# Seven products for eight in the second feed-forward, and two new prices in the planner of a two-layer transformer block

## The chip, the cores and the metric

The kernel runs on one core of a Trainium2 chip. The core has a matrix engine (TensorE, PE in the profile; its weight loads are listed apart as PEld), VectorE (DVE), ScalarE (ACT), GpSimd (POOL) and SyncE (SP), which here issues all transfers. The metric is the device time of one execution in microseconds. Of the kernel before there are three runs: 1750.07, 1753.08 and 1755.17 us, median 1753.08.

## The reference

Two layers work on 512 latent tokens (`x`) and, in the first layer only up to its end, 256 context tokens (`ctx`), with 1024 channels; everything is float32. The mixer has three groups of heads. What matters here is the feed-forward and that layer 1 does it for the latent tokens alone:

```python
def swiglu(h, w1, w3, w2):
    return (jax.nn.silu(h @ w1) * (h @ w3)) @ w2       # 1024 -> 2816 -> 1024

for layer in range(2):
    last = layer == 1
    ...
    x = x + mx[2] * (ox @ w_out[layer])
    x = x + mx[5] * swiglu(modulate(rmsnorm(x, g_ffn[layer]), mx[3], mx[4]), w_ff1[layer], w_ff3[layer], w_ff2[layer])
    if not last:
        ctx = ctx + ...                                # the same for the context tokens
return rmsnorm(x, g_final)
```

## The kernel before

**Products.** A float32 product is made as three fp32r matmuls: each operand is split into a rounded part `hi` and a rest `lo` (a cast on ACT or DVE, then a subtraction on DVE), and hi·hi, hi·lo and lo·hi are added up in PSUM. `split_w` does that for weights. In attention the probabilities are transposed by TensorE (128 rows and columns) and multiplied with the values in plain float32 with 64 output rows, two heads side by side (`pv_pair`, and the same in `attn_c`); such a group is followed by work of 128 output rows again.

**Feed-forward** (from `ncol` to the end of the layer's loop in `dit_block`). The 2816 hidden channels are 22 steps (`FT`) of 128. A step loads and splits the columns of w1 and w3 (`ff_weights`), makes two up projections (`ff_up`, 24 matmuls of 512 columns each in layer 1, where the 512 tokens are the moving side), gates them (`silu` on ACT, product on DVE), and splits the gated tile (`ff_gate`). The down projection of the step before lies between (`ff_w2`, `ff_down`): for each of the four tiles of 128 tokens six matmuls of 512 columns, whose two PSUM tiles DVE adds into the sums `ys`. The last `FF_TAIL` = 3 steps have no down projection in the loop; behind it the sums are gated and added to the residual `xf` (`dve_pool`: VectorE or GpSimd), the w2 rows of those three steps are multiplied by the gate in layer 1 and split, and their down projections end the layer tile by tile. In layer 1 the final norm and the store follow each tile.

**The planner** (class `Plan`). The program records its operations in an order written out by hand, with alternatives of engine where it says so (`act_dve`, `dve_pool`). `schedule` then simulates the five engines with the durations of `price` and takes again and again the operation that can start first; among those of one engine the one earliest in program order, less a `boost` for attention scores and softmax. Several matmuls recorded in `together` are one operation. A transfer may go `lead` operations ahead (`LEAD`), and tiles come from pools with a fixed count (`SLOTS`: 41 tiles of 4 KB in `u`; in PSUM two of two banks, four of one). The order that comes out is the order of each engine's instructions, and all are issued in one line (347), so rows are told apart by tile names: `wh`, `wl` are split weights, `sg` the gated tile, `gh`, `gl` its parts, `y` the sums, `S` and `T` PSUM tiles, `pt` transposed probabilities.

Of the kernel before, what the change touches and what calls it, by code (L numbers as in the profile page):

```python
# [28 lines left out]

ORDER = ["dddd P0 P1 ddddB P2 BABeeeeABAeeeeBABABABeeeeeeeeeCAAAACCCCCC",  # L30
         "P1 P0 B P2 ABBBCAACAABCCCAAB"]
FF_TAIL = 3
FF_ADA = "dddd"
QK_AHEAD = 238
ADA_AHEAD = 300
# [5 lines left out]
COLS = {("a", "q"): (0, 384), ("a", "k"): (384, 128),  # L41
        ("b", "q0"): (640, 128), ("b", "q1"): (768, 128), ("b", "k"): (896, 256),
        ("c", "q"): (1408, 384), ("c", "k"): (1792, 128)}
SA = 0.125
SB = 32.0 ** -0.5
SLOTS = {"u": 41, "pt": 4, "s": 7, "y": 24, "rb": 2, "S": 2, "T": 4, "ropeG": 1}
# [1 line left out]

class _Op:
    __slots__ = ("pos", "alts", "deps", "tiles", "dma", "gate", "tag", "boost",  # L50
                 "users", "left", "banks", "ready", "end", "eng", "calls", "at", "cost", "name")


class _Queue:
# [12 lines left out]
class Plan:  # L67
# [100 lines left out]
    def add(self, alts):  # L168
        op = _Op()
        op.pos, op.tag = len(self.ops), self.label  # L170
        if alts[0][1] is None:
            calls = [o for _, _, o in alts]
            op.alts = [(calls[0][0], sum(self.price(*o) for o in calls), calls)]
        else:
            calls = [alts[0][1]]
            op.alts = [(e, self.price(*c), [c]) for e, c, _ in alts]
        op.dma = calls[0][1] == "dma_start"
        op.gate = op.pos - self.lead if op.dma else 0
        op.boost = 0
        deps, tiles, banks = set(), set(), set()  # L180
        for eng, _, args, kw in calls:
            writes = [args[0]] + ([kw["accum_out"]] if "accum_out" in kw else [])
            reads = [a for a in list(args[1:]) + [v for k, v in kw.items() if k != "accum_out"] if self.is_ap(a)]
            if eng == "pe" and self.label.startswith("att") and self.tile_tag.get(args[0].tensor.name) == "S":
                op.boost = QK_AHEAD
            if not op.dma and self.label in ("ada0", "normA0"):
                op.boost = ADA_AHEAD
            if eng != "pe" and self.label.startswith("att") and any(self.tile_tag.get(a.tensor.name) == "S" for a in reads):
                op.boost = SM_AHEAD
            todo = []  # L190
            if eng == "pe" and kw.get("start", True):

                ws, _ = self.acc.setdefault(args[0].tensor.name, ([], []))
                m = sum(self.banks(args[0]))
                deps.update(o for o, mm in ws if mm & m and o < op.pos and self.ops[o].alts[0][0] == "pe")
            for aps, wr in ((reads, False), (writes, True)):
                for ap in aps:
                    name = ap.tensor.name
                    if name in self.given:
                        continue  # L200
                    m = self.region(ap)
                    if ap.space == PSUM:
                        banks.update((name, b) for b in self.banks(ap))
                    ws, rs = self.acc.setdefault(name, ([], []))
                    deps.update(o for o, mm in ws if mm & m)
                    if wr:
                        deps.update(o for o, mm in rs if mm & m)
                    todo.append((name, m, wr))
            for name, m, wr in todo:
                ws, rs = self.acc[name]  # L210
                if wr:
                    ws[:] = [(o, mm) for o, mm in ws if mm & ~m] + [(op.pos, m)]
                    rs[:] = [(o, mm) for o, mm in rs if mm & ~m]
                else:
                    rs.append((op.pos, m))
                if name in self.tile_tag:
                    tiles.add(name)
        deps.discard(op.pos)
        op.deps, op.tiles, op.banks = deps, tiles, banks
        for t in tiles:  # L220
            self.first.setdefault(t, op.pos)
            self.last[t] = op.pos
        self.ops.append(op)

    def schedule(self):
# [17 lines left out]
        free_at = dict.fromkeys(self.real, 0.0)  # L243
        cand = {e: [] for e in self.real}
        dma_free, now, frontier = 0.0, 0.0, 0
        done, order = [False] * n, []

        bank_end = {}
# [12 lines left out]
        while len(order) < n:  # L261
            best = None
            for e in sorted(free_at, key=free_at.get):
# [51 lines left out]
            if op.dma:  # L315
                free_at[e] = now + 0.5
                dma_free = max(now + 1.4, dma_free) + c
                op.end = dma_free + self.AFTER[e]
            else:
                free_at[e] = now + c  # L320
                op.end = now + c + self.AFTER[e]
            for b in op.banks:
                bank_end.setdefault(b, {})[e] = op.end
            order.append(op)
# [26 lines left out]
def dit_block(  # L351
# [293 lines left out]
    for l in range(2):  # L645
# [646 lines left out]
        def halves(ap):  # L1292
            return [ap[:, 512 * hf:512 * hf + 512] for hf in range(2)]

        ys, gs, ada = {}, [], ada_later()
        for ft in range(FT):
            plan.label = f"ffn{l}"
            plan.lead = LEAD["else"] if ft == 0 else LEAD["ff"]
            ws = ff_weights(ft)
            down = 0 < ft <= FT - FF_TAIL  # L1300
            w2 = ff_w2(ft - 1) if down else None
            for ch in FF_ADA if l == 0 and 1 < ft < FT - FF_TAIL else "":
# [9 lines left out]
            for a in range(2):  # L1312
# [3 lines left out]
                for part in range(1 if last else 2):  # L1316
                    if ft:
                        ff_up(ws[a], s, part)
                    if down:
                        k = 2 * a + part  # L1320
                        for r, i in qtiles[2 * a:2 * a + 2] if last else qtiles[FF_CUT[k]:FF_CUT[k + 1]]:
                            if ft == 1:
                                ys[r, i] = U([1024], name="y")
                            for p, yv in zip(ff_down(gs, [w2], r, i), halves(ys[r, i])):
                                if ft == 1:
                                    act_dve.copy(yv, p)
                                else:
                                    dve.tensor_tensor(yv, p, yv, ALU.add)
                if a == 0:
# [10 lines left out]
        w2s = [ff_w2(ft, gated) for ft in range(FT - FF_TAIL, FT)]  # L1340
        for r, i in qtiles:
            xt = xt0[r, i] = U([1024], name="xf")
            sp.dma_start(xt, xscr[NX * r + i])
            for xv, yv, gate in zip(halves(xt), halves(ys[r, i]), gates[r]):
# [95 lines left out]
```

## Time and profile before

| | |
|---|---|
| runs of the kernel before | 1750.07, 1753.08, 1755.17 us |
| the profiled execution: time / span of its instructions | 1754.11 / 1752.3 us |
| PE busy | 1697.7 us, 97% of the span |
| DVE / ACT / POOL busy | 69% / 35% / 12% |
| mean granted TensorE clock | 0.994 of full speed |

The span of instructions is 1.8 us shorter than the execution. Busy time counts from an instruction's start to its modelled end; instructions of one engine overlap a little, so their pace is read from one start to the next. The layers follow one another: layer 0's attention and projections up to about 470 us, its feed-forward to about 1060, layer 1's attention to about 1345, its feed-forward to the end.

### The profile page before, as it was taken

The page shows a single profiled execution, that of the slowest core. Times are in us where ns is not written, and L with a number is a line of the kernel's source. Part 1 is how long each engine was busy: PE and PEld are TensorE (multiplying, and loading weights), DVE is VectorE, ACT ScalarE, POOL GpSimd, SP SyncE. Part 2 cuts the span into 40 slices and gives each one's busy share as a digit, 9 for nine tenths or more (in the row PEclk, how much of TensorE's full clock was granted, in tenths as well). Part 3 has the DMA queues.
Part 4 walks back from the last instruction along what each step waited for, and adds up shares of the span by engine and source line. Part 5 has one row for each costly group of instructions (what it writes and reads, how often), then busy time and mean ns, then how long its engine had stood idle before and what let it go on. Part 6 is the DMA issues. An engine that isn't in the chain of part 4 may idle for free.

```text
span 1752.3 us, 24291 instructions
## 1 busy us (share of the span) xinstructions
PE 1697.7 (97%) x9426; PEld 1361.3 (78%) x9426; DVE 1208.2 (69%) x1950; ACT 615.2 (35%) x1280; POOL 218.1 (12%) x251
## 2 busy tenths in 40 slices
PE   6999898998999999999999999999999999999998
PEld 3787666676898888888888878877777888888886
DVE  3775878675567887576655765778876666676676
ACT  2523867663342122111101133157674411111111
POOL 0252200011000000000000521542001000000022
PEclk9999999999999999999999999999999999999999
DMA  9502220306363544254232342012005632332341
GB/s 314 188 27 84 67 85 20 96 11 171 96 200 101 169 159 148 93 191 136 69 108 89 105 145 72 13 31 68 1 1 157 180 109 75 106 109 81 112 144 48
DMA packets 153278, 182.96 MB, mean 104 GB/s; under 512 B 9316, under 2 KB 121396, under 8 KB 153164
## 3 DMA queue, kind: packets, MB, share of 16 engines
q1 hardware_dynamic: 153164, 181.42, 33.5%
q8 instruction: 74, 1.21, 0.3%
q14 instruction: 40, 0.33, 0.1%
HBM read 163.00 MB, written 9.47 MB: 98 GB/s over the span
## 4 chain that ended last, share of the span: by engine, by line
PE 86%; DVE 7%; issue 2%; POOL 2%; ACT 2%; DMA 2%; SPq 0%; DVEq 0%; POOLq 0%; ACTq 0%
DMA ws__1259<-in_w_out_dram 1%; PE S__1380 L347 0%; PE S__1379 L347 0%; PE S__1756 L347 0%; PE S__1561 L347 0%; PE S__1628 L347 0%; PE S__1881 L347 0%; PE S__1691 L347 0%; PE S__1823 L347 0%; PE S__1495 L347 0%; PE S__1995 L347 0%; PE S__1393 L347 0%; PE S__1967 L347 0%; PE S__1861 L347 0%; PE S__1853 L347 0%
## 5 line engine op out<-in xcount | busy, mean ns | idle before, releaser
L347 POOL TENSOR_TENSOR y__1397<-y__1397,gate__1998 128x512 f32<-128x512 f32 x1 | 1.3, 1297 | 481.0 <-DVE y__1397 L347 481.0
L347 POOL TENSOR_TENSOR ws__3491<-ws__3491,gate__3490 128x512 f32<-128x512 f32 x1 | 1.3, 1284 | 284.8 <-DMA ws__3491<-in_w_ff_dram 284.8
L347 DVE TENSOR_REDUCE t__2138<-sq__2137 128x6 f32<-128x384 f32 x1 | 0.6, 553 | 19.5 <-ACT sq__2137 L347 19.5
L347 ACT ACT_TABLE_LOAD x6 | 7.7, 1283 | 2.6 <-PE S__3040 L347 1.9
L347 ACT ACTIVATE sg__1860<-S__1853 128x768 f32<-128x768 f32 x1 | 0.8, 812 | 21.2 <-PE S__1853 L347 21.2
L347 ACT ACTIVATE sg__1914<-S__1907 128x768 f32<-128x768 f32 x1 | 0.8, 812 | 21.2 <-PE S__1907 L347 21.2
L347 ACT ACTIVATE sg__1940<-S__1933 128x768 f32<-128x768 f32 x1 | 0.8, 812 | 21.2 <-PE S__1933 L347 21.2
L347 ACT ACTIVATE sg__1966<-S__1959 128x768 f32<-128x768 f32 x1 | 0.8, 812 | 21.2 <-PE S__1959 L347 21.2
L347 DVE TENSOR_TENSOR sg__1994<-sg__1994,S__1995 128x768 f32<-128x768 f32 x1 | 1.0, 955 | 10.3 <-PE S__1995 L347 10.3
L347 ACT ACTIVATE sg__1793<-S__1786 128x768 f32<-128x768 f32 x1 | 0.8, 812 | 17.3 <-PE S__1786 L347 17.3
L347 ACT ACTIVATE sg__1665<-S__1658 128x768 f32<-128x768 f32 x1 | 0.8, 812 | 16.6 <-PE S__1658 L347 16.6
L347 PE MATMUL T__115<-wa__116,cstat 128*32 128x128 f32 x8 | 0.7, 418 | 5.7 <-DMA wa__116<-in_w_ada_dram 5.7
L347 ACT ACTIVATE xn__2033<-xf__2011 128x1024 f32<-128x1024 f32 x1 | 1.1, 1066 | 14.2 <-DVE xf__2011 L347 14.2
L347 POOL TENSOR_TENSOR ropeG<-ropeA,gqk 128x64 f32<-128x64 f32 (+1 forms) x12 | 6.0, 531 | 0.1
L347 ACT ACTIVATE sg__3107<-S__3102 128x512 f32<-128x512 f32 x1 | 0.6, 598 | 14.8 <-PE S__3102 L347 14.8
L347 ACT ACTIVATE sg__3459<-S__3454 128x512 f32<-128x512 f32 x1 | 0.6, 599 | 13.9 <-PE S__3454 L347 13.9
L347 ACT ACTIVATE sg__3173<-S__3168 128x512 f32<-128x512 f32 x1 | 0.6, 598 | 13.8 <-PE S__3168 L347 13.8
L347 ACT ACTIVATE sg__3195<-S__3190 128x512 f32<-128x512 f32 x1 | 0.6, 598 | 13.8 <-PE S__3190 L347 13.8
L347 ACT ACTIVATE sg__3217<-S__3212 128x512 f32<-128x512 f32 x1 | 0.6, 598 | 13.8 <-PE S__3212 L347 13.8
L347 ACT ACTIVATE sg__3239<-S__3234 128x512 f32<-128x512 f32 x1 | 0.6, 598 | 13.8 <-PE S__3234 L347 13.8
L347 ACT ACTIVATE sg__3261<-S__3256 128x512 f32<-128x512 f32 x1 | 0.6, 598 | 13.8 <-PE S__3256 L347 13.8
L347 ACT ACTIVATE sg__3283<-S__3278 128x512 f32<-128x512 f32 x1 | 0.6, 598 | 13.8 <-PE S__3278 L347 13.8
(14035 smaller groups left out, 6711.6 us busy)
## 6 DMA issues: line engine op xcount, KB each, us to landing
x__83<-in_x_dram SPq DMA_DIRECT2D x1, 512.0 KB
x__84<-in_x_dram SPq DMA_DIRECT2D x1, 512.0 KB
x__131<-in_x_dram SPq DMA_DIRECT2D x1, 512.0 KB, 5.9
x__136<-in_x_dram SPq DMA_DIRECT2D x1, 512.0 KB, 6.5
x__198<-in_ctx_dram SPq DMA_DIRECT2D x1, 512.0 KB
x__203<-in_ctx_dram SPq DMA_DIRECT2D x1, 512.0 KB
ws__241<-in_w_in_dram SPq DMA_DIRECT2D x1, 512.0 KB
ws__244<-in_w_in_dram SPq DMA_DIRECT2D x1, 512.0 KB
```

The costliest lines, as they stand in the source:

```text
L347: getattr(self.real[op.eng], method)(*args, **kw)
```

## The change

1. **Down projection of layer 1** (`WINO`). Two steps (256 hidden channels) are taken together. The 512 tokens, the 256 channels and the 1024 outputs are each cut in two, and the product of the 2 x 2 blocks is made by seven block products of sums and differences of blocks (Winograd's form of Strassen's method) in place of eight. Each block product is again three fp32r matmuls for each of two tiles of 128 tokens. The seven products are added up over nine pairs of steps in seven tiles (`wino_y`), and `wino_sum` makes the four blocks of the result from them once. `FF_TAIL` becomes 4 in layer 1, so that 18 steps are taken in pairs.
2. **Planner.** fp32r matmuls are priced (n + 32)/2400 us. `shares_port` names the operations that the planner takes to hold one SBUF port in common (all of GpSimd's; VectorE's with two SBUF inputs, and scalar operations and copies from SBUF to SBUF); the planner lets only one of them run at a time. In attention, a TensorE operation whose count of output rows differs from that of the one before starts 0.095 us later, and operations up to 30 positions behind it may go first.
3. **End of both feed-forwards.** Gating the sums and adding them to the residual is VectorE's alone.

```diff
-FF_TAIL = 3
+FF_TAIL = (3, 4)
+WINO = (1,)
+SWITCH = 0.095
+MODE_AHEAD = 30
...
-                return n / 2400 + 0.003 if n >= 256 else 0.213
+                return (n + 32) / 2400 if n >= 256 else 0.213
...
+    def shares_port(self, eng, method, args, kw):
+        if eng == "pool":
+            return method != "dma_start"
+        if eng != "dve" or method == "memset":
+            return False
+        ins = [a for a in args[1:] if self.is_ap(a) and a.space != PSUM and int(np.prod(a.shape[1:])) > 1]
+        if method.startswith("tensor_scalar") or method == "tensor_copy":
+            return bool(ins) and args[0].space != PSUM
+        return len(ins) > 1
...
+                    if e == "pe" and soon is not None and item[0] > soon[1][0] + MODE_AHEAD and soon[0] <= t0 + SWITCH + 1e-9:
+                        break
...
+                    if e == "pe" and op.mode != mode and op.tag.startswith("att"):
+                        at += SWITCH
+                    if op.port[e]:
+                        at = max(at, port)
...
+        def wino_down(Ge, Go, ft, first):
+            n = ncol // 2
+            nt = n // 128
...
+            def product(form, A, B):
+                (ah, al), (bh, bl) = A, B
+                for t in range(nt):
+                    c = slice(128 * t, 128 * t + 128)
+                    p = PT()
+                    with plan.together():
+                        for k, (a, b) in enumerate(((ah, bh), (ah, bl), (al, bh))):
+                            pe.matmul(p, lhsT=a[:, c], rhs=b, start=(k == 0), stop=(k == 2))
+                    if first:
...
+                        act_dve.copy(wino_y[form, t], p)
+                    else:
+                        dve.tensor_tensor(wino_y[form, t], p, wino_y[form, t], ALU.add)
...
+            sa = split_s(a11, [n])
+            sb = split_s(b11, [512])
+            product(1, sa, sb)
+            yield
+            dve.tensor_tensor(S[:, 0], a21, a22, ALU.add)
+            sub(dve, T[:, 0], b12, b11)
+            sub(dve, S[:, 1], S[:, 0], a11)
+            sub(dve, T[:, 1], b22, T[:, 0])
+            s12, t12 = split_s(S, [2, n]), split_s(T, [2, 512])
+            sub(dve, S3[:, 0], a11, a21)
+            sub(dve, T3[:, 0], b22, b12)
+            sub(dve, S3[:, 1], a12, S[:, 1])
+            sub(dve, T3[:, 1], T[:, 1], b21)
+            product(5, pair(s12, 0), pair(t12, 0))
...
+            product(6, pair(s12, 1), pair(t12, 1))
...
+            s34, t34 = split_s(S3, [2, n]), split_s(T3, [2, 512])
+            product(7, pair(s34, 0), pair(t34, 0))
...
+            so2 = split_s(wo2, [1024])
...
+            product(3, pair(s34, 1), pair(so2, 1))
...
+            sgo = split_s(Go[:, 0:2 * n], [2 * n])
...
+            product(4, pair(sgo, 1), pair(t34, 1))
...
+            product(2, pair(sgo, 0), pair(so2, 0))
...
+        def wino_sum():
+            nt = ncol // 256
+            for t in range(nt):
+                y = [None] + [wino_y[form, t] for form in range(1, 8)]
+                dve.tensor_tensor(y[2], y[1], y[2], ALU.add)
...
+                ys[tiles[t]] = [y[2], y[3]]
+                ys[tiles[nt + t]] = [y[4], y[7]]
...
-            gs = (gs if ft > FT - FF_TAIL else []) + [ff_gate(hs[1], sg)]
+            if l in WINO and ft < FT - tail:
+                dve.tensor_tensor(sg[:, :ncol], sg[:, :ncol], hs[1][:, :ncol], ALU.mult)
+                G.append(sg)
+            else:
+                gs = (gs if ft > FT - tail else []) + [ff_gate(hs[1], sg)]
...
-                dve_pool.tensor_tensor(yv, yv, gate, ALU.mult)
-                dve_pool.tensor_tensor(xv, xv, yv, ALU.add)
+                dve.tensor_tensor(yv, yv, gate, ALU.mult)
+                dve.tensor_tensor(xv, xv, yv, ALU.add)
```

The generator `wino_down` is advanced twice after each up projection, so a pair's seven products stand in the two steps behind it: products 1, 5, 6, 7 in the even step, 3, 4, 2 in the odd one.

## Rows read from the trace of the kernel before

**Rows 1.** The page's part 1: busy us, share of the span and instructions.
```profile
PE 1697.7 (97%) x9426; PEld 1361.3 (78%) x9426; DVE 1208.2 (69%) x1950; ACT 615.2 (35%) x1280; POOL 218.1 (12%) x251
```

**Rows 2.** Busy time by stretch: stretch, its length, PE, PEld, DVE, ACT, POOL, PEclk, DMA share, GB/s.
```profile
100.00:470.00 370.00, 348.87 (x2148) 258.08 (x2147) 254.79 (x498) 204.16 (x534) 64.73 (x74) 0.98 0.26 75
...
970.00:1060.00 90.00, 86.01 (x454) 72.50 (x453) 69.23 (x89) 30.88 (x45) 33.31 (x24) 1.00 0.39 123
1060.00:1345.00 285.00, 279.59 (x1641) 212.18 (x1640) 209.66 (x431) 161.63 (x384) 69.48 (x97) 0.99 0.16 42
...
1400.00:1690.00 290.00, 290.00 (x1281) 240.19 (x1280) 192.92 (x264) 45.68 (x58) 1.28 (x1) 1.00 0.35 109
1690.00:1729.00 39.00, 37.58 (x166) 30.78 (x165) 31.93 (x32) 8.21 (x10) 22.26 (x12) 1.00 0.10 30
1729.00:1753.00 24.00, 16.57 (x74) 13.38 (x72) 13.55 (x23) 5.74 (x16) 2.20 (x4) 0.95 0.23 87
```

**Rows 3.** Timeline of DVE in one step, layer 1's feed-forward: start us, us, what.
```profile
1486.44 1.22 DVE L347 TENSOR_TENSOR wl__3186<-ws__3184,wh__3185 128x1024 fp32r<-128x1024 f32 x1
1487.57 1.22 DVE L347 TENSOR_TENSOR wl__3189<-ws__3187,wh__3188 128x1024 fp32r<-128x1024 f32 x1
1490.90 0.69 DVE L347 TENSOR_TENSOR sg__3173<-sg__3173,S__3174 128x512 f32<-128x512 f32 x1 [2.11 <-PE S__3174 L347]
1491.62 0.43 DVE L347 CAST gh__3179<-sg__3173 128x512 fp32r<-128x512 f32 x1
1492.08 0.69 DVE L347 TENSOR_TENSOR gl__3180<-sg__3173,gh__3179 128x512 fp32r<-128x512 f32 x1
1492.69 0.68 DVE L347 TENSOR_TENSOR y__3063<-T__3175,y__3063 128x512 f32<-128x512 f32 x1
1493.29 0.68 DVE L347 TENSOR_TENSOR y__3063<-T__3176,y__3063 128x512 f32<-128x512 f32 x1
...
1495.08 0.69 DVE L347 CAST wh__3204<-ws__3203 128x1024 fp32r<-128x1024 f32 x1
```

**Rows 4.** Timeline of ACT in the same step.
```profile
1483.23 1.04 ACT L347 CAST wh__3185<-ws__3184 128x1024 fp32r<-128x1024 f32 x1
1484.18 1.04 ACT L347 CAST wh__3188<-ws__3187 128x1024 fp32r<-128x1024 f32 x1
```

**Rows 5.** Timeline of PE in attention: entries to and exits from 64 rows.
```profile
194.29 0.65 PE L347 MATMUL T__433<-pt__435,V__214 128*64 128x256 f32 x4
...
1201.32 0.27 PE L347 MATMUL T__2436<-ident,P__2419 128*128 128x128 f32 x1
1201.52 0.65 PE L347 MATMUL T__2427<-pt__2435,V__2114 128*64 128x256 f32 x4
1202.11 0.33 PE L347 MATMUL T__2438<-ident,P__2398 128*128 128x128 f32 x1
...
1204.08 0.65 PE L347 MATMUL T__2427<-pt__2437,V__2115 128*64 128x256 f32 x4
1204.56 0.60 PE L347 MATMUL T__2427<-pt__2439,V__2115 128*64 128x256 f32 x4
...
1334.40 0.44 PE L347 MATMUL T__2921<-pt__2933,V__2115 128*64 128x256 f32 x2
```

**Rows 6.** Timeline of DVE at the end of layer 1's feed-forward.
```profile
1700.36 2.31 DVE L347 TENSOR_TENSOR wl__3472<-ws__3470,wh__3471 128x1024 fp32r<-128x1024 f32 x1
...
1717.99 1.21 DVE L347 TENSOR_TENSOR wl__3483<-ws__3481,wh__3482 128x1024 fp32r<-128x1024 f32 x1
1719.12 1.77 DVE L347 TENSOR_TENSOR xf__3502<-xf__3502,y__3063 128x512 f32<-128x512 f32 x1
1720.82 0.68 DVE L347 TENSOR_TENSOR xf__3503<-xf__3503,y__3066 128x512 f32<-128x512 f32 x1
```

**Rows 7.** Timeline of POOL in the same stretch.
```profile
1698.07 1.29 POOL L347 TENSOR_TENSOR ws__3494<-ws__3494,gate__3489 128x512 f32<-128x512 f32 x1
1699.32 2.27 POOL L347 TENSOR_TENSOR ws__3494<-ws__3494,gate__3490 128x512 f32<-128x512 f32 x1
```

More of the change, by code (lines that the diff above doesn't have):

```diff
@@ L50 @@
     __slots__ = ("pos", "alts", "deps", "tiles", "dma", "gate", "tag", "boost",
-                 "users", "left", "banks", "ready", "end", "eng", "calls", "at", "cost", "name")
+                 "users", "left", "banks", "ready", "end", "eng", "calls", "at", "cost", "name", "mode", "port")
 class _Queue:
@@ L176, in add @@
             op.alts = [(e, self.price(*c), [c]) for e, c, _ in alts]
+        op.mode = calls[0][2][0].shape[0] if calls[0][0] == "pe" else 0
+        op.port = {a[0]: self.shares_port(*(a[1] or calls[0])) for a in alts}
         op.dma = calls[0][1] == "dma_start"
@@ L245, in schedule @@
         dma_free, now, frontier = 0.0, 0.0, 0
+        mode, port = 128, 0.0
         done, order = [False] * n, []
@@ L321, in schedule @@
                 op.end = now + c + self.AFTER[e]
+            if e == "pe":
+                mode = op.mode
+            if op.port[e]:
+                port = now + c
             for b in op.banks:
@@ L1293, in halves, with split_s, pair @@
             return [ap[:, 512 * hf:512 * hf + 512] for hf in range(2)]
+        def split_s(src, shape):
+            hi = U(shape, F32R, "fh")
+            act_dve.copy(hi, src)
+            lo = U(shape, F32R, "fl")
+            sub(dve, lo, src, f(hi))
+            return hi, lo
+        def wino_down(Ge, Go, ft, first):
+            n = ncol // 2
+            nt = n // 128
+            raws2 = []
+            for k in range(2):
+                w = U([1024], name="w2")
+                sp.dma_start(w, w_ff2[l, 128 * (ft + k):128 * (ft + k) + 128, :])
+                raws2.append(w)
+            we, wo2 = raws2
+            a11, a21, a12, a22 = Ge[:, 0:n], Ge[:, n:2 * n], Go[:, 0:n], Go[:, n:2 * n]
+            b11, b12, b21, b22 = we[:, 0:512], we[:, 512:1024], wo2[:, 0:512], wo2[:, 512:1024]
+            def product(form, A, B):
+                (ah, al), (bh, bl) = A, B
+                y = None
+                for t in range(nt):
[5 more added lines that the diff above has]
+                    if first:
+                        if t % 2 == 0:
+                            y = U([2, 512], name="yw")
+                        wino_y[form, t] = y[:, t % 2]
+                        act_dve.copy(wino_y[form, t], p)
+                    else:
+                        dve.tensor_tensor(wino_y[form, t], p, wino_y[form, t], ALU.add)
+            def pair(h, j):
+                return h[0][:, j], h[1][:, j]
+            sa = split_s(a11, [n])
+            sb = split_s(b11, [512])
+            product(1, sa, sb)
+            yield
+            S, T = U([2, n], name="S12"), U([2, 512], name="T12")
+            dve.tensor_tensor(S[:, 0], a21, a22, ALU.add)
[3 more added lines that the diff above has]
+            s12, t12 = split_s(S, [2, n]), split_s(T, [2, 512])
+            S3, T3 = U([2, n], name="S34"), U([2, 512], name="T34")
+            sub(dve, S3[:, 0], a11, a21)
[3 more added lines that the diff above has]
+            product(5, pair(s12, 0), pair(t12, 0))
+            yield
+            product(6, pair(s12, 1), pair(t12, 1))
+            yield
+            s34, t34 = split_s(S3, [2, n]), split_s(T3, [2, 512])
+            product(7, pair(s34, 0), pair(t34, 0))
+            yield
+            so2 = split_s(wo2, [1024])
+            so2 = [h.rearrange("p (j n) -> p j n", j=2) for h in so2]
+            product(3, pair(s34, 1), pair(so2, 1))
+            yield
+            sgo = split_s(Go[:, 0:2 * n], [2 * n])
+            sgo = [h.rearrange("p (j n) -> p j n", j=2) for h in sgo]
+            product(4, pair(sgo, 1), pair(t34, 1))
+            yield
+            product(2, pair(sgo, 0), pair(so2, 0))
+            yield
@@ new lines, in wino_sum @@
+        def wino_sum():
[3 more added lines that the diff above has]
+                dve.tensor_tensor(y[2], y[1], y[2], ALU.add)
+                dve.tensor_tensor(y[6], y[1], y[6], ALU.add)
+                dve.tensor_tensor(y[7], y[6], y[7], ALU.add)
+                dve.tensor_tensor(y[6], y[6], y[5], ALU.add)
+                dve.tensor_tensor(y[3], y[6], y[3], ALU.add)
+                sub(dve, y[4], y[7], y[4])
+                dve.tensor_tensor(y[7], y[7], y[5], ALU.add)
+                ys[tiles[t]] = [y[2], y[3]]
+                ys[tiles[nt + t]] = [y[4], y[7]]
@@ L1295, in dit_block @@
+        wino_y, wino, G = {}, None, []
+        tail = FF_TAIL[l]
         ys, gs, ada = {}, [], ada_later()
@@ L1299, in dit_block @@
             ws = ff_weights(ft)
-            down = 0 < ft <= FT - FF_TAIL
+            down = 0 < ft <= FT - tail and l not in WINO
+            if l in WINO and 0 < ft <= FT - tail and ft % 2 == 0:
+                wino = wino_down(*G, ft - 2, ft == 2)
+                G = []
             w2 = ff_w2(ft - 1) if down else None
-            for ch in FF_ADA if l == 0 and 1 < ft < FT - FF_TAIL else "":
+            for ch in FF_ADA if l == 0 and 1 < ft < FT - tail else "":
                 plan.label, plan.lead, ada_eng[0] = "ada1", LEAD["ada"], ch
@@ L1328, in dit_block @@
                                     dve.tensor_tensor(yv, p, yv, ALU.add)
+                    for _ in range(2 if last else 1):
+                        next(wino, None) if wino else None
                 if a == 0:
@@ L1331, in dit_block @@
                     act.activation(sg[:, :ncol], s[:, :ncol], AF.Silu)
-            gs = (gs if ft > FT - FF_TAIL else []) + [ff_gate(hs[1], sg)]
+            if l in WINO and ft < FT - tail:
[3 more added lines that the diff above has]
+                gs = (gs if ft > FT - tail else []) + [ff_gate(hs[1], sg)]
+        if wino:
+            for _ in wino:
+                pass
+            wino_sum()
+        else:
+            ys = {k: halves(y) for k, y in ys.items()}
         for _ in ada if not last else ():
@@ L1339, in dit_block @@
         gated = [(slice(512 * hf, 512 * hf + 512), gates[0][hf]) for hf in range(2)] if last else None
-        w2s = [ff_w2(ft, gated) for ft in range(FT - FF_TAIL, FT)]
+        w2s = [ff_w2(ft, gated) for ft in range(FT - tail, FT)]
         for r, i in qtiles:
@@ L1343, in dit_block @@
             sp.dma_start(xt, xscr[NX * r + i])
-            for xv, yv, gate in zip(halves(xt), halves(ys[r, i]), gates[r]):
-                dve_pool.tensor_tensor(yv, yv, gate, ALU.mult)
-                dve_pool.tensor_tensor(xv, xv, yv, ALU.add)
+            for xv, yv, gate in zip(halves(xt), ys[r, i], gates[r]):
+                dve.tensor_tensor(yv, yv, gate, ALU.mult)
+                dve.tensor_tensor(xv, xv, yv, ALU.add)
         if not last:
```

## The prediction

> **What bounds the kernel now.** I read the page first: PE is busy 97% of the span, no other engine over 69% [rows 1]. An average can hide stages that something else limits, so the busy time by stretch came next. In layer 1's feed-forward (1400 to 1690 us) PE is busy all of 290.00 us with 1281 matmuls, one every 290.00 / 1281 = 0.2264 us, at full clock; DVE is at 192.92 / 290 = 67%, ACT at 16%, transfers at 0.35. In the attention stretches PE is still busy 348.87 of 370 us and 279.59 of 285 us [rows 2]. So time goes away where TensorE gets less to do, or stops less, as long as DVE keeps up; DVE's and ACT's prices were then read from the timeline of one step [rows 3, 4], TensorE's changes of tiling from that of attention [rows 5], and what DVE and POOL do to each other from the end of the layer [rows 6, 7].
>
> **Seven products: what TensorE saves.** A pair of steps had 2 x 24 = 48 down matmuls of 512 columns; now it has 7 products x 2 tiles x 3 = 42. Nine pairs save 54, all of the form that streams at 0.2264 us: 54 x 0.2264 = 12.2 us. The four tail steps still have 24 each; the up projections stay. Nothing on TensorE is added.
>
> The Trainium skill ("Trainium Kernel Development and Optimization", Performance Expectations) holds TensorE's matmul busy share for a bad measure of what is left, and the share of weight loads for a good one. By it this stretch stands at 240.19 / 290 = 83% and the cut would give 0.83 x 12.2 = 10.1 us; the trace's even pace of starts [rows 2] speaks for 12.2, which I use.
>
> **What DVE gets for it, per pair.** Prices from start to start: addition from PSUM into `y` (512 columns) 0.60, `lo` of 1024 columns 1.13, of 512 0.61, gate 0.72 [rows 3]. For 256 columns, which these rows lack, I estimate 0.34 (half of 0.61 and a little), between 0.30 and 0.61.
> - before: 192.92 / 290 of a pair of 144 x 0.2264 = 32.6 us, so 21.7 us.
> - after: 14 additions 8.4 (16 before); four `lo` of w1 and w3 4.5; two gates 1.4; the sums of blocks, four of 512 and four of 256 columns, 2.4 + 1.4 = 3.8; the `lo` of the blocks, three of 1024, four of 512 and one of 256 columns, 3.4 + 2.4 + 0.3 = 6.1. Together 24.2 us in a pair of 138 x 0.2264 = 31.2 us: 78%.
> - the `hi` casts: 9472 columns a pair. ACT takes 0.95 us for 1024 [rows 4], 8.8 us in all, which its 16% leaves room for.
>
> It is uneven. The even step has four products, all sums and most splits: 4.8 + 2.3 + 0.7 + 3.8 + 4.4 = 16.0 us of DVE beside 72 x 0.2264 = 16.3 us of PE. The odd step has 3.6 + 2.3 + 0.7 + 1.7 = 8.3 beside 14.9. All that hangs on w2 alone (the `T` sums and their splits) can be done in the odd step before, and TensorE has 24 up matmuls that need no product to go on with. The new wait, gate of the odd tile, two sums, cast, `lo` (0.72 + 0.68 + 0.5 + 0.6 = 2.5 us), has 6 + 24 + 6 matmuls of PE, 8.1 us, ahead of product 5, which uses it. Behind late sums on DVE stand the additions that empty the four `T` tiles, and TensorE would wait for those. The w2 rows are the same bytes on SP's queue, two together at the even step's start in place of one a step, and the sums hold seven `u` tiles in place of four: with transfers at 0.35 I cost that at nothing; if a row came late, the up matmuls would cover it. So 0 lost here. Bounds: 0, and DVE setting the even step: its casts too (5888 columns x 0.69 / 1024 = 4.0 us [rows 3]) make 20.0 us, 3.7 over, 33 us in nine pairs.
>
> **The end of layer 1.** DVE gets `wino_sum`, 14 x 0.60 = 8.4 us, the gating and `lo` of a fourth w2 step, 2.3, and POOL's 12 instructions of that stretch [rows 2], 12 x 0.60 = 7.2. But POOL's help was dear: a `lo` of 1024 columns takes 2.31 us beside POOL and 1.21 alone, an addition of 512 1.77 and 0.68 [rows 6], and POOL's own go from 1.29 to 2.27 [rows 7]; nine DVE instructions between 1697 and 1721 us are stretched so, two of them shown, by about 1.0 each. Net 8.4 + 2.3 + 7.2 - 9 = 9 us more on DVE, where it has 39 - 31.93 = 7 us free and the tail's 24 - 13.55 = 10 [rows 2], and 5.4 us of matmuls move into that tail. Gating the sums now runs beside the tail's first tiles. I take +1 us; bounds 0 and +9.
>
> **The end of layer 0** has the same edit. DVE is busy 69.23 of 90 us there and PE idle for 4 [rows 2]; what POOL's work costs DVE and what its absence gives back are like amounts. 0; bounds -4 and +4.
>
> **The planner's prices.** Elsewhere only the order changes. Entering 64 output rows costs 0.20 us in place of the transposes' 0.11, leaving them 0.59 in place of 0.48 between two such groups: 0.20 us for both [rows 5]. The 170 groups (92 in layer 0, 78 in layer 1, counted in the loops) stand in 116 runs, the first and last of which are in [rows 5]: 23 us. PSUM has four `T` tiles, one the accumulator, and `pt` four tiles, so that runs of three are about the most: 57 runs, 59 x 0.20 = 11.8 us less. Half of that seems likely, since scores still break in between and some of the time becomes waiting: -6. The port's price keeps DVE and POOL apart in the plan, which on the chip they are anyway [rows 6, 7]; where POOL gives work to DVE, it comes out even. The dearer matmul (0.2267 for 512 columns) is what rows 2 show. Bounds: -18 (all 11.8, and a quarter of PE's 26 us of pauses in attention [rows 2]) and +12 (each of 35 attention units a third of a us later).
>
> **The sum.** -12.2 + 0 + 1 + 0 - 6 = -17.2. The profiled execution took 1754.11 us: 1736.9. The median of the runs is 1.0 lower: **1736 us**.
>
> **The rivals.**
> - *The products' gain alone.* The planner breaks runs but pays in waits. For it: each step is chosen for the earliest start, so an operation held back gains nothing by itself. 1754.1 - 12.2 + 1 - 1.0 = 1742.
> - *Attention gives the gain back.* Values are multiplied later, `pt` and `T` stay taken, and each of 35 units ends a third of a us later: +12, in place of -6. For it: ACT and DVE are at 55 to 74% there [rows 2], with chains through all three engines. Against: PE is busy 94 to 98%. 1754.1 - 12.2 + 12 + 1 - 1.0 = 1754.
> - *Slower: DVE sets the even step.* Place: products 5 to 7, with `u` too full for work ahead and the casts on DVE. Price as above 33 us: 1754.1 - 12.2 + 33 - 6 + 1 - 1.0 = 1769. It decides once DVE is late by 17.2 / 9 = 1.9 us a pair. Against: 7 us a pair are free on it, and ACT is idle most of the time.
> - *The planner does nothing*: runs stay at 116. That is the first rival's time.
>
> **How the numbers follow.** The forecast 0.60, the products' gain alone 0.21, attention gives it back 0.09, DVE sets the step 0.10. What a measurement of this kernel tells from no change is about 0.3%, 5.3 us: faster is under 1747.8, slower over 1758.3. The first two are faster (0.81), the third the same (0.09), the last slower (0.10). The range reaches from -29 us, the planner's and layer 0's better bounds without their last 5, to the edge of the third case: 1724 to 1752.
>
> **What would show it.** Right: in layer 1's feed-forward PE busy all the time at 0.226 us a matmul, 54 matmuls fewer; a pair of steps 31.2 us; DVE 75 to 90% there; 60 to 90 runs of 64 rows; no DVE addition of 1.77 us at the layers' ends; a tail without a pause over 2 us. Wrong: PE waiting on DVE's `lo` or `y` in the even steps; the same number of runs; attention stretches longer than 370 and 285 us; a pause before the tail's third tile.

## The result, and the profile after

The changed kernel takes **1731.09 us** (1729.83 to 1732.49 in four runs) and the kernel before, in the same comparison, 1754.12: a ratio of 0.9871 with a 95% interval of 0.9849 to 0.9892. That is 23 us less; 17 were forecast, and the time lies in the range. The profiled span falls from 1752.3 to 1728.0 us. Page, part 1, of the changed kernel:

```profile
PE 1676.6 (97%) x9372; PEld 1354.1 (78%) x9372; DVE 1235.6 (72%) x2108; ACT 660.8 (38%) x1337; POOL 116.8 (7%) x170
```

TensorE has 54 matmuls fewer and is busy 97% of the span as before; GpSimd is busy 117 us in place of 218 [rows 1]. Its stretches (columns as in [rows 2]); they begin earlier, so the borders are shifted:

```profile
100.00:464.00 364.00, 343.93 (x2137) 256.55 (x2136) 250.11 (x521) 201.93 (x522) 38.53 (x59) 0.98 0.26 76
...
960.00:1052.00 92.00, 90.57 (x480) 77.28 (x479) 70.95 (x110) 32.84 (x48) 3.81 (x5) 1.00 0.40 130
1052.00:1335.00 283.00, 274.92 (x1638) 212.77 (x1637) 206.68 (x459) 162.03 (x384) 46.07 (x67) 0.99 0.17 42
...
1390.00:1666.00 276.00, 276.00 (x1220) 228.53 (x1219) 224.06 (x325) 84.88 (x116) 2.99 (x2) 1.00 0.36 109
1666.00:1705.00 39.00, 39.00 (x174) 32.30 (x173) 38.70 (x57) 10.83 (x14) 1.46 (x1) 1.00 0.29 97
1705.00:1728.00 23.00, 16.20 (x72) 13.09 (x70) 10.97 (x19) 5.47 (x16) 2.20 (x4) 0.96 0.24 92
```

In layer 1's feed-forward TensorE still does not stop: 276.00 us with 1220 matmuls are 0.2262 us each, as before [rows 2]. VectorE goes from 67 to 224.06 / 276 = 81%, and in front of the tail it is busy 38.70 of 39 us. Yet from 1390 us to the end the view of waits has no row for TensorE, where before it waited 1.4 us for VectorE's gate of the last step but one:

```profile
PE S__3486 L347 <- DVE sg__3474 L347: 1.4, 1, 1.4
```

VectorE in an even step of the changed kernel, around the sums of blocks (`yw` are the sums of the seven products, `S__3290`, `T__3291` and their like here the sums of blocks in SBUF, `fh` and `fl` their `hi` and `lo`):

```profile
1521.36 0.68 DVE L375 TENSOR_TENSOR yw__3111<-T__3274,yw__3111 128x512 f32<-128x512 f32 x1
1521.96 0.41 DVE L375 TENSOR_TENSOR S__3290<-sg__3246,sg__3271 128x256 f32<-128x256 f32 x1
1522.29 1.21 DVE L375 TENSOR_TENSOR fl__3295<-T__3291,fh__3294 128x1024 fp32r<-128x1024 f32 x1
1523.42 0.42 DVE L375 TENSOR_TENSOR S__3290<-S__3290,sg__3246 128x256 f32<-128x256 f32 x1
1523.76 1.21 DVE L375 TENSOR_TENSOR fl__3307<-T__3297,fh__3306 128x1024 fp32r<-128x1024 f32 x1
```

From start to start the sum of 256 columns takes 0.33 and the addition `yw` of 512 columns 0.60 us, the `lo` of 1024 columns 1.13: the prices of [rows 3], and the estimate of 0.34. At the end of the layer:

```profile
1664.30 2.37 DVE L375 TENSOR_TENSOR yw__3082<-yw__3066,yw__3082 128x512 f32<-128x512 f32 x2
...
1669.01 2.32 DVE L375 TENSOR_TENSOR wl__3551<-ws__3549,wh__3550 128x1024 fp32r<-128x1024 f32 x1
...
1692.48 1.22 DVE L375 TENSOR_TENSOR wl__3584<-ws__3582,wh__3583 128x1024 fp32r<-128x1024 f32 x1
1693.61 0.68 DVE L375 TENSOR_TENSOR xf__3585<-xf__3585,yw__3111 128x512 f32<-128x512 f32 x1
```

GpSimd still does three gates of w2 rows there (the 2.99 and 1.46 us in its column above), and beside them one of two additions and a `lo` are stretched: 2.37 us for two additions that take 1.28 elsewhere, and 2.32. From 1671 us on none is: 1.22 in place of 2.31, 0.68 in place of 1.77 [rows 6]. In attention groups of 64 rows stand together more often than before: in TensorE's timeline 45 of 89 runs hold a single group, 87 of 121 did in the kernel before, and 9 hold four to six, as here:

```profile
1190.13 0.65 PE L375 MATMUL T__2427<-pt__2433,V__2114 128*64 128x256 f32 x4
1190.61 0.60 PE L375 MATMUL T__2427<-pt__2435,V__2114 128*64 128x256 f32 x4
1191.04 0.60 PE L375 MATMUL T__2427<-pt__2437,V__2115 128*64 128x256 f32 x4
1191.47 0.60 PE L375 MATMUL T__2427<-pt__2439,V__2115 128*64 128x256 f32 x4
```

So the runs fall by 32, from 121 to 89; the prediction's count of 116 for the kernel before is 5 too low.

How much each stage gave is read from two rows of TensorE's timeline, the last transpose ahead of layer 1's feed-forward and the last matmul of all. Before, then after:

```profile
1387.69 0.60 PE L347 MATMUL T__3032<-ident,xn__3026 128*128 128x128 f32 x4
...
1745.19 0.39 PE L347 MATMUL T__3526<-wh__3498,gl__3488 128*128 128x512 f32 x1
```

```profile
1377.31 0.60 PE L375 MATMUL T__3032<-ident,xn__3026 128*128 128x128 f32 x4
...
1720.81 0.39 PE L375 MATMUL T__3611<-wh__3583,gl__3570 128*128 128x512 f32 x1
```

The stage takes 1745.19 - 1387.69 = 357.50 us before and 1720.81 - 1377.31 = 343.50 after: 14.0 us. What lies ahead of it got 10.4 us shorter.

### The profile page after: what moved, and what is told of

Read it like the earlier page. It is cut to its first block, busy times and chain, and to the rows that moved or that the text cites. A ratio compares the mean times of both kernels' runs of the same rounds, so it can differ in the third digit from the quotient of the medians.

```text
span 1728.0 us, 24300 instructions
## 1 busy us (share of the span) xinstructions
PE 1676.6 (97%) x9372; PEld 1354.1 (78%) x9372; DVE 1235.6 (72%) x2108; ACT 660.8 (38%) x1337; POOL 116.8 (7%) x170
## 4 chain that ended last, share of the span: by engine, by line
PE 75%; DVE 3%; ACT 2%; DMA 1%; issue 0%; SPq 0%; POOL 0%; DVEq 0%; POOLq 0%; ACTq 0%
DMA ws__2960<-in_w_out_dram 1%; PE S__1380 L375 0%; PE S__1379 L375 0%; PE S__1756 L375 0%; PE S__1628 L375 0%; PE S__1561 L375 0%; PE S__1881 L375 0%; PE S__1691 L375 0%; PE S__1823 L375 0%; PE S__1495 L375 0%; PE S__1995 L375 0%; PE S__1993 L375 0%; PE S__1984 L375 0%; PE S__1393 L375 0%; PE S__1861 L375 0%; PE S__1853 L375 0%
## 5 line engine op out<-in xcount | busy, mean ns | idle before, releaser
L375 ACT ACTIVATE sg__1468<-S__1461 128x768 f32<-128x768 f32 x1 | 0.8, 812 | 21.2 <-PE S__1461 L375 21.2
L375 ACT ACTIVATE sg__1914<-S__1907 128x768 f32<-128x768 f32 x1 | 0.8, 812 | 21.2 <-PE S__1907 L375 21.2
L375 ACT ACTIVATE sg__1940<-S__1933 128x768 f32<-128x768 f32 x1 | 0.8, 812 | 21.2 <-PE S__1933 L375 21.2
L375 ACT ACTIVATE sg__1860<-S__1853 128x768 f32<-128x768 f32 x1 | 0.8, 812 | 21.2 <-PE S__1853 L375 21.2
L375 ACT ACTIVATE sg__1966<-S__1959 128x768 f32<-128x768 f32 x1 | 0.8, 812 | 21.2 <-PE S__1959 L375 21.2
L375 ACT ACTIVATE sg__1665<-S__1658 128x768 f32<-128x768 f32 x1 | 0.8, 812 | 17.8 <-PE S__1658 L375 17.8
L375 ACT ACTIVATE sg__1793<-S__1786 128x768 f32<-128x768 f32 x1 | 0.8, 812 | 17.8 <-PE S__1786 L375 17.8
L375 ACT ACTIVATE sg__1598<-S__1591 128x768 f32<-128x768 f32 x1 | 0.8, 812 | 11.9 <-PE S__1591 L375 11.9
L375 ACT ACTIVATE sg__1763<-S__1756 128x768 f32<-128x768 f32 x1 | 0.8, 812 | 11.1 <-PE S__1756 L375 11.1
L375 ACT ACTIVATE sg__1568<-S__1561 128x768 f32<-128x768 f32 x1 | 0.8, 812 | 11.1 <-PE S__1561 L375 11.1
L375 ACT ACTIVATE sg__1635<-S__1628 128x768 f32<-128x768 f32 x1 | 0.8, 812 | 11.1 <-PE S__1628 L375 11.1
L375 ACT ACTIVATE sg__1830<-S__1823 128x768 f32<-128x768 f32 x1 | 0.8, 812 | 11.1 <-PE S__1823 L375 11.1
L375 ACT ACTIVATE sg__1888<-S__1881 128x768 f32<-128x768 f32 x1 | 0.8, 812 | 10.9 <-PE S__1881 L375 10.9
L375 ACT ACTIVATE sg__1698<-S__1691 128x768 f32<-128x768 f32 x1 | 0.8, 812 | 10.9 <-PE S__1691 L375 10.9
```

The source lines that it names most:

```text
L375: getattr(self.real[op.eng], method)(*args, **kw)
```

## The experiments

Each kernel was timed in five rounds against the kernel before. "Stage" is the time between the two rows just shown, "ahead" the time of the first of them, in one profiled execution each. The ratios are to the kernel before as timed beside each kernel; its median was 1752.7 to 1753.7 us beside e1 to e14.

| kernel | us | ratio to before, 95% | ahead | stage |
|---|---|---|---|---|
| before | 1754.12 | 1 | 1387.7 | 357.5 |
| changed | 1731.09 | 0.9871 (0.9849 to 0.9892) | 1377.3 | 343.5 |
| e1 products only | 1751.66 | 0.9992 (0.9983 to 1.0001) | 1384.4 | 357.5 |
| e9 products, gating by VectorE | 1744.64 | 0.9949 (0.9937 to 0.9962) | 1385.0 | 350.9 |
| e14 products, no GpSimd at the end | 1738.03 | 0.9915 (0.9901 to 0.9928) | 1386.0 | 343.5 |
| e2 planner and gating only | 1744.06 | 0.9951 (0.9939 to 0.9964) | 1377.6 | 355.7 |
| e10 port and matmul price only | 1748.34 | 0.9970 (0.9958 to 0.9982) | 1383.0 | 355.7 |
| e13 tiling price only | 1759.60 | 1.0043 (1.0031 to 1.0056) | 1397.4 | 357.5 |
| e3 changed, no tiling price | 1735.81 | 0.9904 (0.9891 to 0.9918) | 1382.0 | 343.5 |
| e4 changed, no port | 1754.60 | 1.0011 (1.0002 to 1.0020) | 1396.8 | 349.6 |
| e11 changed, neither | 1753.45 | 1.0006 (0.9997 to 1.0015) | 1396.1 | 347.7 |
| e5 changed, gating by either | 1731.63 | 0.9874 (0.9859 to 0.9890) | 1378.7 | 344.0 |
| e7 changed, tail of two | 1740.94 | 0.9935 (0.9923 to 0.9948) | 1379.6 | 352.4 |
| e8 products in both layers | 1740.84 | 0.9925 (0.9912 to 0.9937) | 1389.4 | 343.5 |

The kernel before, e1, e9 and e14 have the same order on TensorE up to layer 1's feed-forward and still differ by 3.3 us in "ahead", so a difference there of one or two us says nothing. "Stage" is steadier: the five kernels with the products and no pause in it agree to 0.5 us.

**e1: the seven products alone.** The changed kernel with the planner and the gating of before:

```diff
-SWITCH = 0.095
+SWITCH = 0.0
...
     def shares_port(self, eng, method, args, kw):
-        if eng == "pool":
-            return method != "dma_start"
-        if eng != "dve" or method == "memset":
-            return False
+        return False
...
-                return (n + 32) / 2400 if n >= 256 else 0.213
+                return n / 2400 + 0.003 if n >= 256 else 0.213
...
-                dve.tensor_tensor(yv, yv, gate, ALU.mult)
-                dve.tensor_tensor(xv, xv, yv, ALU.add)
+                dve_pool.tensor_tensor(yv, yv, gate, ALU.mult)
+                dve_pool.tensor_tensor(xv, xv, yv, ALU.add)
```

> The seven products alone: the new down projection of layer 1 with the planner's prices of before (no price of a tiling change, no shared port, the cheaper matmul, gating by VectorE or GpSimd). Theory A, the two halves of the change add up and the products give what TensorE no longer does, 12 to 14 us: about 1741 us, and PE busy all through layer 1's feed-forward. Rival B, the products only fit because the new planner keeps VectorE and GpSimd apart and TensorE's price is right: VectorE, at 97% in the even step by count, falls behind, PE has pauses there, and the time is over 1747.

Measured 1751.66 us, so theory A fell as it stood: by themselves the products give next to nothing, the stage is as long as before. But rival B's place was wrong too. The long waits of TensorE from 1390 us on are in front of the tail, not in the even steps:

```profile
PE T__3592 L372 <- DVE gh__3569 L372: 5.5, 1, 5.5
PE T__3592 L372 <- DVE gl__3559 L372: 2.0, 1, 2.0
```

Behind them stand VectorE's `gl` and `gh` of the last steps. VectorE's timeline, then GpSimd's:

```profile
1694.08 1.21 DVE L372 TENSOR_TENSOR wl__3562<-ws__3560,wh__3561 128x1024 fp32r<-128x1024 f32 x1
...
1701.03 1.21 DVE L372 TENSOR_TENSOR wl__3581<-ws__3579,wh__3580 128x1024 fp32r<-128x1024 f32 x1
1702.16 0.67 DVE L372 TENSOR_TENSOR sg__3556<-sg__3556,S__3557 128x512 f32<-128x512 f32 x1
1702.76 1.72 DVE L372 TENSOR_TENSOR wl__3584<-ws__3582,wh__3583 128x1024 fp32r<-128x1024 f32 x1
1710.76 1.73 DVE L372 TENSOR_TENSOR gl__3559<-sg__3556,gh__3558 128x512 fp32r<-128x512 f32 x1 [6.28 <-POOL xf__3586 L372]
```

```profile
1694.23 9.16 POOL L372 TENSOR_TENSOR yw__3111<-yw__3111,gate__3571 128x512 f32<-128x512 f32 x1 [11.90 <-ACT sg__3556 L372]
1703.36 2.27 POOL L372 TENSOR_TENSOR yw__3101<-yw__3101,gate__3572 128x512 f32<-128x512 f32 x1
```

GpSimd's gating of 128 x 512, an operation of 1.29 us where nothing holds it up [rows 7], takes 9.16 us. All that while VectorE runs one instruction after another with SBUF operands alone, nine from 1694.08 us on, and GpSimd ends 1.2 us after VectorE turns to the gate at 1702.16, which reads PSUM. The planner had counted on 1.2 us. Everything behind it on GpSimd is late, and `gl__3559` waits 6.28 us for GpSimd. The Trainium skill (SBUF — State Buffer, "SBUF: two separate sides") says the port pair of the two engines is an exclusive lock held for a whole instruction, the loser blocked; the rows agree, and show that the loser can lose many times in a row. The pause costs twice. By stretch, columns as in [rows 2]:

```profile
1700.00:1710.00 10.00, 10.00 (x46) 8.25 (x45) 4.48 (x4) 1.12 (x2) 9.92 (x6) 1.00 0.00 0
1710.00:1720.00 10.00, 2.58 (x7) 1.24 (x5) 9.17 (x10) 0.00 (x0) 5.22 (x4) 0.63 0.00 1
1720.00:1730.00 10.00, 9.90 (x31) 7.87 (x32) 4.33 (x8) 1.44 (x4) 0.55 (x1) 0.69 0.05 17
```

TensorE's granted clock is 0.63 and 0.69 in the two stretches behind the start of the pause, partly the lower of its two levels of 1.2 and 2.4 GHz; with 9.90 us busy it gets through 31 matmuls, where at 2.4 GHz 46 fit in 10.

**e2: the planner and the gating alone.** `WINO = ()`, `FF_TAIL = (3, 3)`, the rest as changed.

> The planner's new prices and the gating by VectorE alone, with the down projection of before in both layers. Theory A: layer 1's feed-forward was reached 10.4 us earlier in the changed kernel's trace than before, and 1.4 us of pause at its end went too; both stay here: 1754 - 11 to 12 = about 1742. Rival B: a good part of that is bound to the whole change (another order by chance), and this is over 1748.

Measured 1744.06, -9 us: theory A, with a gain a little below its 11 to 12. The rows that mark its stage:

```profile
1377.57 0.60 PE L375 MATMUL T__3032<-ident,xn__3026 128*128 128x128 f32 x4
...
1733.31 0.39 PE L375 MATMUL T__3526<-wh__3498,gl__3488 128*128 128x512 f32 x1
```

It takes 355.74 us, 1.8 less than before (the pause of 1.4 at the layer's end is gone). From here to the changed kernel only the products differ: 355.74 - 343.50 = **12.2 us**, the 54 x 0.2264 of the prediction.

**e9 and e14: what GpSimd costs the products.** e9 is e1 with gating by VectorE alone; e14 also takes from GpSimd the gate on the tail's w2 rows:

```diff
         for part, s in scale or ():
-            dve_pool.tensor_tensor(st[:, part], st[:, part], s, ALU.mult)
+            dve.tensor_tensor(st[:, part], st[:, part], s, ALU.mult)
```

> The products alone once more, but with VectorE alone gating the sums and adding them to the residual (the planner's prices stay those of before). The products-alone run lost 7.5 us in front of the tail, where TensorE waited for VectorE and that for GpSimd's gating, one instruction of which took 9.16 us, and TensorE's clock was low behind it. Theory G, that gating is what ate the products' gain: the pause goes and the time is 1741 to 1743. Rival B, GpSimd's other work at the end (the gate on the rows of w2) and the old prices do it too: 1746 or more.

> The products with the planner's prices of before, and VectorE alone for both kinds of work that GpSimd had at the end of layer 1: gating the sums, and the gate on the last rows of w2 (eight instructions). With the port's price this stage took 343.2 us from the last transpose to the last matmul, without it 350.6 even with the gating on VectorE. Theory G, it is GpSimd's work beside VectorE's at the end that costs the difference: the stage falls to 343 to 345 and the run to 1737 to 1740. Rival B, the order made with the old prices costs it in the even steps: the stage stays over 348, the run over 1742.

e9 takes 1744.64 us, between the two figures: gating was about half of it. e14 takes 1738.03, and its stage is that of the changed kernel, with the old prices in the planner:

```profile
1385.97 0.60 PE L372 MATMUL T__3032<-ident,xn__3026 128*128 128x128 f32 x4
...
1729.46 0.39 PE L372 MATMUL T__3611<-wh__3583,gl__3570 128*128 128x512 f32 x1
```

1729.46 - 1385.97 = 343.49 us. So theory G is shown: the products' 12.2 us, and the pause of before with them, come in full as soon as GpSimd does no gating at the layer's end, with the planner's old prices too. The price of the port does for this stage what those eight plus the gating edits do by hand, although it leaves GpSimd three of the eight.

**e5: gating by either engine in the changed kernel.** 

> The changed kernel with gating by VectorE or GpSimd, as the planner chooses, as before the change. Theory P, the port's price already keeps GpSimd out of it: four of GpSimd's instructions differ, and the time is within 2 us of 1731. Rival G, it is the gating's place that matters: a pause in front of the tail and 1735 or more.

1731.63 us, theory P: once the port has a price, the edit of the gating makes no difference that these runs show.

**e3, e4, e11, e10, e13: the planner's prices apart.** e3 has `SWITCH = 0.0`, e4 `shares_port` returning False, e11 both; e10 and e13 are the kernel before with the port's and the matmul's price, and with the tiling price.

> The changed kernel with a price of zero for a change of tiling (nothing else). Theory S, the earlier arrival at layer 1's feed-forward comes from fewer runs of 64 rows: the runs go back from 84 to about 116, 32 x 0.20 = 6.4 us come back, 1737 to 1738. Rival P, it comes from keeping VectorE and GpSimd apart: the runs go back, but the time stays within 2 us of 1731.

> The changed kernel with no operation taken to share a port (nothing else; gating stays VectorE's). Theory S: time within 2 us of 1731, runs of 64 rows stay near 84. Rival P: GpSimd gets its work of before (busy over 150 us in place of 117), stretched VectorE rows come back in projections and stacking, and 4 to 8 us come back: 1735 to 1739.

> The changed kernel without the port's price and without the price of tiling: the dearer matmul, the gating by VectorE and the products stay. Without the port alone layer 1's stretch from the norm to the first product with values took 162.0 us in place of 149. Theory C, that was the price of tiling in a plan without the port: 150 to 152 us here, and about 1745 in all. Rival M, it was the dearer matmul in such a plan, which shifts work to GpSimd: 160 or more here, 1752 or more.

> The kernel before with the shared port and the new price of a matmul in the planner, and nothing else (no products, no price for tiling, gating by VectorE or GpSimd). Theory P, the port carries most of the planner's gain: GpSimd's busy time falls from 218 to about 120 us, layer 1's feed-forward starts 5 to 6 us earlier, and the stretched VectorE rows at both ends go: 1745 to 1748. Rival S, the price of tiling changes carries it: 1751 or more.

> The kernel before with the price of a change of tiling, and nothing else. Theory A, the prices add up: the runs of 64 rows fall from 116 to 80 to 90, layer 1's attention gets some 7 us shorter, 1746 to 1748. Rival C, the price of tiling only pays in a plan that also knows the shared port, as without it the changed kernel's order took 12 us longer between the norm and the first product with values of layer 1: 1753 or more, although the runs fall as well.

Without the tiling price 4.7 us come back (e3), and the runs go to 125: nearer to theory S. But without the port 23.5 us come back (e4), more than either theory had, although the runs stay at 86. Of these, 6 are in the stage of the products; most of the rest lies between layer 0's end and layer 1's first product with values. There, in e4 and then in the changed kernel:

```profile
1032.00:1145.00 113.00, 107.24 (x481) 88.03 (x480) 79.71 (x151) 36.12 (x68) 43.01 (x47) 0.97 0.23 72
1145.00:1194.00 49.00, 42.42 (x207) 32.55 (x206) 39.09 (x85) 30.25 (x80) 17.15 (x26) 0.93 0.14 34
```

```profile
1027.00:1132.00 105.00, 103.57 (x477) 85.17 (x476) 71.61 (x166) 38.67 (x73) 17.74 (x20) 1.00 0.25 79
1132.00:1176.00 44.00, 40.72 (x210) 32.45 (x210) 36.27 (x83) 30.88 (x83) 15.31 (x25) 0.96 0.16 37
```

162 us against 149, GpSimd busy 60 against 33. TensorE waits there for the scaling of a row tile (`xn__2065`), which takes 1.75 us in e4 and 0.75 in the changed kernel; but it takes 1.75 in the kernel before as well, whose stretch is 150.3 us, so this row does not explain e4. From the kernel before, port and matmul price alone give 5.4 us (e10, at the upper edge of theory P; GpSimd's busy time falls from 218 to 133 us):

```profile
PE 1700.7 (97%) x9426; PEld 1362.1 (78%) x9426; DVE 1189.3 (68%) x2009; ACT 619.1 (35%) x1285; POOL 133.2 (8%) x187
```

The tiling price alone makes it **6.9 us slower** (e13), though the runs fall to 89: theory A fell and rival C's time was right. Added to port and matmul price, with the gating, it gives 3 to 4 us (e10 to e2). So the prices do not add up; fewer runs helped only in a plan with the port's price. Rival C's mechanism fell, though: e11, without both, should have lost nothing between the norm and the first product with values, and that stretch takes 157.6 us (162.0 in e4, 150.3 before). Rival M, the dearer matmul in a plan without the port, has the time right and most of the stretch. Two kernels at hand bear it out: e9 and e11 differ in the matmul's price alone. The first transpose and the first product with values of layer 1, in e9 and then in e11:

```profile
1030.74 0.27 PE L372 MATMUL T__2045<-ident,xn__2033 128*128 128x128 f32 x1
...
1182.27 0.65 PE L372 MATMUL T__2376<-pt__2378,V__2113 128*64 128x256 f32 x4
```

```profile
1033.68 0.27 PE L372 MATMUL T__2045<-ident,xn__2033 128*128 128x128 f32 x1
...
1191.24 0.65 PE L372 MATMUL T__2376<-pt__2378,V__2113 128*64 128x256 f32 x4
```

The stretch takes 151.5 us in e9 and 157.6 in e11, and the whole 8.8 us more (1744.64, 1753.45). M's reason, work shifted to GpSimd, is not shown: GpSimd has 70 instructions in that stretch in both. Which wait of the new order costs it stays open, and so does why e13 is slow: all its stretches ahead of layer 1's feed-forward are longer than before, by 0.2 to 4 us, with no single pause to name (its profiled execution took 1763.81 us, 4.2 over its median). The port's price without the dearer matmul was not tried.

**e7: a tail of two steps.** `FF_TAIL = (3, 2)`.

> The changed kernel with a tail of two steps in place of four in layer 1, so that a tenth pair is made by seven products. Six matmuls less are 6 x 0.2264 = 1.4 us. Theory A, TensorE sets the pace to the end: 1729.7. Rival D, VectorE, busy 38.7 of 39 us in front of the tail, has no room: the sum of the blocks can begin only behind the last step, with 10.9 us of matmuls as cover in place of 21.7 and more, TensorE waits there, 1733 or more.

1740.94 us, rival D. The wait in front of the tail's third tile and the stretches:

```profile
PE T__3630 L375 <- DVE xf__3611 L375: 7.6, 1, 7.6
```

```profile
1700.00:1710.00 10.00, 10.00 (x46) 8.26 (x45) 10.00 (x17) 0.60 (x1) 0.00 (x0) 1.00 0.01 2
1710.00:1720.00 10.00, 7.10 (x30) 5.10 (x28) 10.00 (x17) 0.62 (x1) 0.00 (x0) 1.00 0.00 0
1720.00:1730.00 10.00, 4.77 (x14) 3.84 (x15) 8.90 (x16) 3.29 (x10) 0.55 (x1) 0.66 0.01 2
```

VectorE has 10.00 us of work in each 10, TensorE stops for 7.6 us, and its granted clock falls behind it. A tail of two steps does not cover `wino_sum`; one of four does.

**e8: seven products in layer 0 too.** `WINO = (0, 1)`, `FF_TAIL = (4, 4)`.

> The changed kernel with seven products in layer 0 as well (768 tokens, three tiles for each product, tail of four steps). Per pair 63 matmuls in place of 72, nine pairs: 81 x 0.2264 = 18.3 us. Theory A, TensorE sets the pace there too and VectorE has room (68% busy now, some 82% by count): 1731 - 18 = 1713, a microsecond or two more for the pause at the layer's end. Rival B, VectorE also makes layer 1's modulation in that stretch, and 14 tiles of sums in place of 6 leave too little of the 41 for work ahead: pauses on TensorE, over 1722.

1740.84 us, 10 more than the changed kernel: rival B, and worse. The longest of TensorE's waits, one of VectorE's, and two stretches of layer 0's feed-forward, with layer 1's modulation beside it and without:

```profile
PE S__1906 L375 <- DVE wl__1898 L375: 2.2, 1, 2.2
```

```profile
DVE acc__1709 L375 <- DMA wa__1712<-in_w_ada_dram: 2.5, 1, 2.5
```

```profile
620.00:670.00 50.00, 46.83 (x265) 38.81 (x263) 45.41 (x57) 11.47 (x13) 0.00 (x0) 1.00 0.39 117
...
920.00:970.00 50.00, 50.00 (x277) 43.73 (x276) 36.73 (x52) 11.60 (x13) 0.00 (x0) 1.00 0.21 64
```

At 620 us TensorE is busy 46.83 of 50 and VectorE 45.41; at 920, with the modulation done, 50.00 and 36.73. VectorE's modulation waits for its weights, which come late, and the `lo` of w1 and w3 behind it are late for TensorE. That the tiles of sums leave too few of the 41 for loads ahead fits, but the two causes were not tried apart. Neither e7 nor e8 beats the changed kernel.

## Why the prediction was right, point by point

**The products, -12.2 us: right.** e2 and the changed kernel differ by 12.2 us in the stage. The share of weight loads, which the Trainium skill (Trainium Kernel Development and Optimization, Performance Expectations) names as a good measure, would have given 10.1 in the way the prediction turned it into a price; the measurement decides for the even pace of starts. VectorE's load was forecast at 24.2 us of 31.2, 78%; with some casts it is 81%, and no even step made TensorE wait.

**The end of layer 1, +1 us: wrong sign, -1.8.** The step that failed is "Net 8.4 + 2.3 + 7.2 - 9 = 9 us more on DVE [...] I take +1 us". The load was there: 38.70 of 39 us busy. But the sum left out the kernel before's own pause of 1.4 us, which came from the same stretched instructions and went with them, and TensorE found its operands in time. One of the prediction's signs failed here too: not every stretched addition went, as the port's price leaves GpSimd three gates in front of the tail. Also unseen: this term is the condition of the first. With GpSimd at the end as before, the products' gain is eaten entirely (e1); I had the two engines cost each other some 1.0 us an instruction, and it can be 8.

**The planner, -6 us: near in size, in part by luck and for the wrong reason.** By the timed runs e2 gives 9 us, 1.8 of them in the stage, so some 7 ahead of it, 1.4 of these at layer 0's end (below). The single profiles, less sure there, have 10; but 3.8 of it lies in layer 0's attention (289.4 us from the first product with values to the feed-forward before, 285.6 changed), where e1, with the order of the kernel before, has 285.9. The step that failed is "The port's price keeps DVE and POOL apart in the plan, which on the chip they are anyway [...] it comes out even": the port and matmul price alone give 5.4 us, and without the port nothing of the whole change is left. The dearer matmul was put at nothing as well, and without the port it costs 8.8 us (e9 to e11). The runs did fall, to 89, inside 60 to 90, and in a plan with the port's price the tiling price is worth 4.7 us (e3), not far from the 6. But against the kernel before little of that is left: layer 1's attention, from its first to its last product with values, takes 149.7 us before, 153.6 in e3 and 147.9 changed. The same fall without the port's price goes with 6.9 us lost. So of the 6 us that the forecast lacked, 2.8 are at layer 1's end and 1.4 at layer 0's; the rest is ahead of the stage, spread over the attention of both layers, and too small to be told apart in single profiles.

**The end of layer 0, 0 us: -1.4, inside the bounds.** From the first matmul of layer 0's feed-forward to layer 1's first transpose it takes 551.0 us before and in e1, and 549.6 in e9, which has e1's prices and gating by VectorE; e10, with the port's price and gating by either engine, has 549.6 too.

The rival "attention gives the gain back" was no idle one: e13 is that case, in a plan without the port.

## What to carry to other kernels

Cutting TensorE's work paid here only where the engine that gets the extra work was not also blocked by a neighbour: look at what runs beside it at the end of the stage, and try giving that to the blocked engine itself. In a planner that did not know that two engines exclude each other, two other prices, each read from rows, made the kernel slower (e13, e9 to e11); I would put that price first, though it was not tried alone. A saving that depends on another part of a change is found only by running each part alone.

## What the runs showed of the hardware

- GpSimd can lose the port to VectorE for many instructions in a row (nine in e1, 9.16 us for work of 1.29), while in the kernel before the two took turns (VectorE 1.77, GpSimd 2.27 [rows 6, 7]); what decides between the two was not tried.
- The pauses of TensorE in e1 (2.0 and 5.5 us) and e7 (7.6 us) were paid once more by its clock: 0.63 to 0.69 granted in the 20 us from their start in e1, 0.66 from 1720 to 1730 us in e7.
- A change to 64 output rows and back costs 0.20 us [rows 5]; four groups in a row start 0.43 to 0.48 us apart and pay it once.
